# Attention rows in class order: queries, keys, values, bias rows and finished rows, the last pair's sums turned by products, weight splits in halves

## The chip, the cores and the metric

The kernel runs on one core of a Trainium2 chip. The metric is the device time of one execution in microseconds (us); the kernel before takes 1211.53 us, the median of three runs.

## What is computed

One decoder layer on 1024 rows of 1024 numbers: a projection feeds a dilated attention of eight heads and a gated recurrence (HGRN2) of four heads; their outputs are joined, projected, added to x, and a two-layer network with a squared ReLU follows. The part around the change is the attention:

```python
DILATED_PATTERNS = ((128, 1), (512, 4), (2048, 16))
...
def dilated_mixture_attention(q, k, v, slopes):
    outs, lses = [], []
    for window, dilation in DILATED_PATTERNS:
        o, lse = dilated_branch(q, k, v, slopes, window, dilation)
        outs.append(o)
        lses.append(lse)
    w = jax.nn.softmax(jnp.stack(lses, axis=0), axis=0)
    return jnp.sum(w[..., None] * jnp.stack(outs, axis=0), axis=0)
```

A query sees near keys one by one, and farther keys only in steps of 4. A row's *class* is its number modulo 4 (`DIL`): far keys of a query are those of its class.

## The kernel before

Products of fp32 numbers are made of three passes (`three_pass`, L89): each operand is split into a high part, copied by ACT, and the rest, subtracted on DVE (`split_into`, L85). Weights stream through two raw buffers: `w_split` (L110) takes the next tile, ACT writes its high part, DVE its low part, and SP then issues the load of the next but one. `w_get(i, ahead)` (L132) splits up to tile i + ahead. For the output weights the gain is folded in (L124, L125).

The program is recorded in order, each engine runs its own instructions in that order, and waits are made from the data and from the buffers. It has three stages: the four recurrence heads (to about 300 us), the attention (to about 520 us), and the output projection with the two-layer network. All of PE's long work lies in one queue of generators; `fill` (L179) takes pieces from it between the pieces of attention, so that PE has projections to run while other engines work.

The attention of eight heads is a loop of 64 steps (L1275), eight per head: `ITEMS` (L1269) are four diagonal blocks D0 to D3 of the first 512 queries, two far steps F0, F1 and two near steps N0, N1 of the last 512. A step raises the next item's scores to exponentials (`raise_`, ACT), looks at later scores (`look`: products on PE into tile ps, bias and minimum on DVE, a D3 look being 512 columns wide), turns its own block by PE (`turn`: tile pt, then high part pth on ACT and rest ptl on DVE), weighs values with what the step before turned (`weigh`: tile pov), and finishes what was weighed before (`finish`: o on DVE). `fill` runs in the middle and at the end; `hooks` (L1243) adds work of certain steps: splits of output weights, and `row_turn`, which turns finished rows of the recurrence (tile pmt, split into emt).

Two heads share one projection, a *pair*. `attn_proj` (L738) makes queries, values and keys of a pair in two halves of 512 rows: rows are scaled by rrow (the row's norm), written to a half buffer (qf, vf, kf; two such buffers, `half`, L60), split by ACT and POOL (q and ql, kh and kl), and parts are copied across by DMA. Keys and values are put in class order when they are scaled; queries and rrow stand in row order. So far queries are gathered with a step of four (`far_queries`, L860), the near scores' turned tile pt_N is read with a step of four (L929), and the far output is added to row order (L987, L1002). Far denominators reach row order through DRAM (`send`, `receive`), the minimum over both kinds by a small product (`swap_low`, tile px) with picking tiles pick4 and pick32.

When a pair is done, `pair_turn` (tile pot, two halves) and `pair_rows` (anat) bring it back to rows and store it (L1035). This happens in the first three steps of the next pair (L1294, L1327 to L1331). The last pair (`LASTP`) is turned and scaled inside `finish` (L1011 to L1017). PSUM tiles take turns in pairs of banks by tag; pot, pt and pmt share the two of tag t.

## Time and profile before

| | us |
|---|---|
| median of 3 runs (1211.53 to 1212.24) | 1211.53 |
| the profiled execution | 1211.33 |
| its span | 1209.5 |
| PE busy in the span | 1196.5 |
| DVE busy | 861.4 |
| ACT busy | 548.8 |
| POOL busy | 307.4 |

The granted clock of TensorE is full in the whole span. PE's matmuls are pipelined and their ends are modelled, so a busy PE is read with care: a 512-column matmul is shown with 0.39 us, but in an unbroken row the next begins about 0.23 us after it. The idle time of another engine costs nothing as long as PE has work.

### The profile page before, as it was taken

The page shows a single profiled execution, that of the slowest core. Times are in us where ns is not written, and L with a number is a line of the kernel's source. Part 1 is how long each engine was busy: PE and PEld are TensorE (multiplying, and loading weights), DVE is VectorE, ACT ScalarE, POOL GpSimd, SP SyncE. Part 2 cuts the span into 40 slices and gives each one's busy share as a digit, 9 for nine tenths or more (in the row PEclk, how much of TensorE's full clock was granted, in tenths as well). Part 3 has the DMA queues.
Part 4 walks back from the last instruction along what each step waited for, and adds up shares of the span by engine and source line. Part 5 has one row for each costly group of instructions (what it writes and reads, how often), then busy time and mean ns, then how long its engine had stood idle before and what let it go on. Part 6 is the DMA issues. An engine that isn't in the chain of part 4 may idle for free.

```text
span 1209.5 us, 17110 instructions
## 1 busy us (share of the span) xinstructions
PE 1196.5 (99%) x6326; PEld 1023.9 (85%) x6326; DVE 861.4 (71%) x1436; ACT 548.8 (45%) x1067; POOL 307.4 (25%) x287
## 2 busy tenths in 40 slices
PE   9999999999999998999999999999999999999998
PEld 8898989888888887888888888888888888888886
DVE  5697878777667767676689566766678554478796
ACT  7633333322665667765664222222234543534562
POOL 0120212022221110144330786575631000000022
PEclk9999999999999999999999999999999999999999
DMA  5231323123544446173514555553587534433337
GB/s 219 70 93 58 97 83 97 48 82 87 139 99 118 126 124 163 42 243 116 192 61 157 183 194 192 202 182 143 203 320 261 207 100 143 161 100 104 105 105 278
DMA packets 86467, 172.38 MB, mean 143 GB/s; under 512 B 13424, under 2 KB 39024, under 8 KB 86384
## 3 DMA queue, kind: packets, MB, share of 16 engines
q1 hardware_dynamic: 86384, 171.29, 43.5%
q8 instruction: 50, 0.82, 0.3%
q14 instruction: 33, 0.27, 0.1%
HBM read 116.98 MB, written 47.99 MB: 136 GB/s over the span
## 4 chain that ended last, share of the span: by engine, by line
PE 95%; ACT 2%; DVE 1%; issue 1%; DMA 0%; SPq 0%; POOL 0%; DVEq 0%; POOLq 0%; ACTq 0%
PE f L1976 18%; PE f2s L1976 7%; PE pig L92 2%; PE pig L90 2%; PE pig L91 2%; PE pl L488 2%; PE pwo L91 2%; PE pwo L92 2%; PE pwo L90 2%; PE pm_f L90 1%; PE pm_ak L90 1%; PE pm_f L92 1%; PE pm_aq L90 1%; PE pm_f L91 1%; PE pm_aq L92 1%; PE pm_ak L92 1%
## 5 line engine op out<-in xcount | busy, mean ns | idle before, releaser
L87 DVE TENSOR_TENSOR al<-ar,ah 128x1024 fp32r<-128x1024 f32 x56 | 70.6, 1261 | 80.0 <-ACT ah L86 77.6
L1976 PE MATMUL f<-bh,ah 128*128 128x512 f32 x320 | 124.5, 389 | 0.0
L1976 PE MATMUL f<-bl,ah 128*128 128x512 f32 x320 | 124.5, 389 | 0.0
L1976 PE MATMUL f<-bh,al 128*128 128x512 f32 x320 | 124.5, 389 | 0.0
L86 ACT ACTIVATE ah<-ar 128x1024 fp32r<-128x1024 f32 x56 | 59.2, 1057 | 86.9 <-DMA ar<-actd 86.0
L1976 PEld LDWEIGHTS f<-bh,al 128*128 128x128 f32 x320 | 60.1, 188 | 12.6
L1976 PEld LDWEIGHTS f<-bh,ah 128*128 128x128 f32 x320 | 60.1, 188 | 12.5
L1976 PEld LDWEIGHTS f<-bl,ah 128*128 128x128 f32 x320 | 60.1, 188 | 12.3
L2050 POOL TENSOR_SCALAR lbl<-ssq 128x1 f32<-128x1 f32 x4 | 3.3, 821 | 244.9 <-ACT fd L2046 244.8
L1599 POOL TENSOR_TENSOR e<-x,e 128x512 f32<-128x512 f32 x14 | 21.6, 1540 | 131.8 <-DVE x L1550 131.8
L1976 PE MATMUL f2s<-bh,al 128*128 128x512 f32 (+1 forms) x128 | 48.9, 382 | 0.0
L1976 PE MATMUL f2s<-bl,ah 128*128 128x512 f32 (+1 forms) x128 | 48.9, 382 | 0.0
L1976 PE MATMUL f2s<-bh,ah 128*128 128x512 f32 (+1 forms) x128 | 48.9, 382 | 0.0
L717 POOL TENSOR_TENSOR kl<-kf,kh 64x512 fp32r<-64x512 f32 x16 | 22.2, 1391 | 97.0 <-ACT kh L716 82.1
L681 POOL TENSOR_SCALAR tout<-traw 128x256 f32<-128x256 f32 x16 | 19.1, 1196 | 103.1 <-DMA traw<-in_bias_tab_dram 72.1
L87 DVE TENSOR_TENSOR bl<-br,bh 128x1024 fp32r<-128x1024 f32 x32 | 40.1, 1253 | 1.6 <-ACT bh L86 1.5
L1993 ACT ACTIVATE acc<-f 128x512 f32<-128x512 f32 x28 | 16.7, 598 | 48.7 <-PE f L1976 48.7
L761 POOL TENSOR_TENSOR ql<-qf,q 64x512 fp32r<-64x512 f32 x16 | 21.4, 1337 | 62.8 <-ACT q L760 62.2
L86 ACT ACTIVATE bh<-br 128x1024 fp32r<-128x1024 f32 x32 | 33.6, 1050 | 4.8 <-PE f L1976 4.2
L87 DVE TENSOR_TENSOR wl<-raw,wh 128x1024 fp32r<-128x1024 f32 x21 | 25.9, 1233 | 9.1 <-ACT wh L86 9.1
L90 PE MATMUL pwo<-woh,mt 128*128 128x512 f32 x80 | 32.2, 402 | 0.0
L91 PE MATMUL pwo<-wol,mt 128*128 128x512 f32 x80 | 31.3, 391 | 0.0
(1706 smaller groups left out, 3966.5 us busy)
## 6 DMA issues: line engine op xcount, KB each, us to landing
ar<-actd SPq DMA_DIRECT2D x56, 512.0 KB, 3.6
br<-in_w_ff_dram SPq DMA_DIRECT2D x16, 1024.0 KB, 6.0
w1r<-in_w_ff_dram SPq DMA_DIRECT2D x14, 1024.0 KB, 6.5
raw<-in_w_in_dram SPq DMA_DIRECT2D x26, 512.0 KB, 3.7
actd<-e SPq DMA_DIRECT2D x17, 768.0 KB, 4.2
actd<-e SPq DMA_DIRECT2D x11, 1024.0 KB, 4.1
raw<-in_w_out_dram SPq DMA_DIRECT2D x8, 512.0 KB, 4.0
xres<-in_x_dram SPq DMA_DIRECT2D x8, 512.0 KB, 4.5
```

Source lines behind the costliest of these rows:

```text
L86: S.activation(hi, src, AF.Copy)
L87: eng.tensor_tensor(out=lo, in0=src, in1=f32(hi), op=ALU.subtract)
L90: TE.matmul(dst, lhs[0], rhs[0], start=start, stop=False)
L91: TE.matmul(dst, lhs[0], rhs[1], start=False, stop=False)
L92: TE.matmul(dst, lhs[1], rhs[0], start=False, stop=stop)
L488: TE.matmul(pl[:, n % 2, :192], kt[:, n * P:(n + 1) * P], sets[u // 2][:, n % 4], start=True, stop=True)
L681: G.tensor_scalar(by_class(dst[:, part_ * w:(part_ + 1) * w]), in_blocks(raw[:, FAR * DIL:]), -1.0, None, op0=ALU.mult)
L717: G.tensor_tensor(out=kl[a:b], in0=src, in1=f32(kh[a:b]), op=ALU.subtract)
L761: G.tensor_tensor(out=lo[a:b], in0=full[a:b], in1=f32(stacks[i]["q"][a:b, sl]), op=ALU.subtract)
L1599: eng[0].tensor_tensor(out=e1[:, 3], in0=a21, in1=e1[:, 2], op=ALU.add)
L1976: TE.matmul(pm, a[:, j, c], b[:, j, d], start=start and j == 0 and q == 0, stop=stop and j == 1 and q == 2, skip_group_check=True)
L1993: S.activation(acc_at(p, i), pm, AF.Copy)
```

## The change

Queries of a block of 128 rows now stand in class order, like the keys and values. The row scale rrow is put in class order once, in place, by ACT, while pair 0's queries are projected (a copy to a half buffer, a copy back, for each half). Bias rows are loaded in class order by four DMAs for one, the far denominators are received by four, and a finished pair's rows are stored in row order by four. `far_queries` and the near tiles then read runs of 32. The last pair returns to row order inside `weigh`, and its sums by a product with a permuting tile (`in_order`), whose tile POOL makes from the identity.

The order of the steps changes too: at the pair ends `turn` comes before the second `pair_turn`, and the second `pair_rows` directly after `finish`; `far_queries` comes after `finish`; at step 42 the weight split comes before the key copy; two weight splits (steps 48 and 55) are made in halves in two steps (`wo_half`).

```diff
+    def wo_half(k, c):
+        i = WO0 + k
+        sl = slice(c * 512, c * 512 + 512)
...
+        gain = gcols[:, k:k + 1]
+        S.activation(parts[i][0][:, sl], raws[i][:, sl], AF.Copy, scale=gain)
+        V.scalar_tensor_tensor(parts[i][1][:, sl], raws[i][:, sl], gain, f32(parts[i][0][:, sl]),
+                               op0=ALU.mult, op1=ALU.subtract)
+        if c == 1:
+            raws.pop(i)
+            done[1] += 1
+            w_load()
...
+        near_cols = bias_tab[hd][:, T - NEAR + part_ * w:T - NEAR + (part_ + 1) * w].rearrange("(i r) c -> r i c", r=DIL)
+        for r in range(DIL):
+            nc.sync.dma_start(out=raw[32 * r:32 * r + 32, FAR * DIL:], in_=near_cols[r])
...
-        V.tensor_tensor(out=full.rearrange("p (r m) -> p m r", r=DIL), in0=pm.rearrange("p (m r) -> p m r", r=DIL),
-                        in1=rrow[:, sl].rearrange("p (m r) -> p m r", r=DIL), op=ALU.mult)
+        V.tensor_tensor(out=full.rearrange("p (r m) -> p r m", r=DIL), in0=classes(pm),
+                        in1=rrow[:, sl].rearrange("p (r m) -> p r m", r=DIL), op=ALU.mult)
...
+                if pr == 0 and n == 2:
+                    moved = half(f"rc{hf}")
+                    S.activation(moved.rearrange("p (r m) -> p r m", r=DIL), classes(rrow[:, sl]), AF.Copy)
+                    S.activation(rrow[:, sl], moved, AF.Copy)
...
-            V.scalar_tensor_tensor(full, box[0], -0.125, rrow[:, sl], op0=ALU.mult, op1=ALU.mult)
+            V.scalar_tensor_tensor(full.rearrange("p (r m) -> p r m", r=DIL), classes(box[0]), -0.125,
+                                   rrow[:, sl].rearrange("p (r m) -> p r m", r=DIL), op0=ALU.mult, op1=ALU.mult)
...
-                S.activation(stacks[i]["q"][a:b, sl], full[a:b], AF.Copy)
-                G.tensor_tensor(out=lo[a:b], in0=full[a:b], in1=f32(stacks[i]["q"][a:b, sl]), op=ALU.subtract)
+                src = full[a:b].rearrange("p (r j i) -> p j r i", r=DIL, i=32)
+                S.activation(by_class(stacks[i]["q"][a:b, sl]), src, AF.Copy)
+                G.tensor_tensor(out=by_class(lo[a:b]), in0=src, in1=by_class(f32(stacks[i]["q"][a:b, sl])), op=ALU.subtract)
...
-        S.activation(st["q"], q[:, 512:].rearrange("p (m r) -> p r m", r=DIL), AF.Copy)
+        S.activation(st["q"].rearrange("p r (j i) -> p r j i", i=32),
+                     q[:, 512:].rearrange("p (j r i) -> p r j i", r=DIL, i=32), AF.Copy)
...
-        if kind == "D" and g % 2:
+        if kind == "D" and g % 2 and hd // 2 < LASTP:
             V.reciprocal(st["rd"][:, g - 1:g + 1], st["dn"][:, g - 1:g + 1])
...
+    def in_order(hd, a, b, pS):
+        TE.matmul(pS[:, :b - a], early["order"], stats[hd]["dn"][:, a:b],
+                  start=True, stop=True)
+        return pS[:, :b - a]
...
+        if kind == "D":
+            sums = in_order(hd, b0, b0 + 2, po)
...
+        G.tensor_copy(early["order"].rearrange("p (i r) -> p i r", r=DIL), ident.rearrange("p (r i) -> p i r", r=DIL))
...
-        42: lambda: w_get(WO0, 0),
...
-        48: lambda: [values_turn("t"), w_split()],
-        49: lambda: load_bias(AH - 1),
+        48: lambda: [values_turn("t"), wo_half(3, 0)],
+        49: lambda: [wo_half(3, 1), load_bias(AH - 1)],
...
-        55: lambda: [w_get(WO0 + 4, 0), row_load(0)],
+        55: lambda: [wo_half(4, 0), row_load(0)],
+        56: lambda: wo_half(4, 1),
...
+        turn(hd, kind, g)
+        raise_(*coming, which=(1,))
         if s % 16 == 2 and s > 16:
             pair_turn(s // 16 - 1, 1)
-        turn(hd, kind, g)
-        raise_(*coming, which=(1,))
-        if i == 0:
-            far_queries(hd)
...
+        if s % 16 == 2 and s > 16:
+            pair_rows(s // 16 - 1, 1)
         if i == 0:
+            far_queries(hd)
             spread_low(hd, 0)
...
+        if s == 42:
+            w_get(WO0, 0)
         if i in (1, 2, 3, 6, 7):
             key_job()
```

How the change moves instructions, at three places. ACT, where pair 0's queries begin (wh is a weight tile's high part, q the queries' high parts); before:

```order
L1238 ACTIVATE texp<-nhalf 128x1
L86 ACTIVATE wh_2694<-raw_2454 128x1024
L760 ACTIVATE q_0_2709<-qf_2711 64x512
L760 ACTIVATE q_1_2710<-qf_2711 64x512
L760 ACTIVATE q_0_2709<-qf_2770 64x512
```

and now:

```order
L1289 ACTIVATE texp<-nhalf 128x1
L774 ACTIVATE rc_2732<-rrow 128x512
L775 ACTIVATE rrow<-rc_2732 128x512
L86 ACTIVATE wh_2741<-raw_2498 128x1024
L786 ACTIVATE q_0_2756<-qf_2758 64x512
L786 ACTIVATE q_1_2757<-qf_2758 64x512
L774 ACTIVATE rc_2788<-rrow 128x512
L775 ACTIVATE rrow<-rc_2788 128x512
L786 ACTIVATE q_0_2756<-qf_2820 64x512
```

Two copies of rrow stand ahead of the weight split, two more between the two halves of the queries.

ACT at step 42, where the first output weight is split (kh are keys' high parts, pf exponentials); before:

```order
L716 ACTIVATE kh_1_4636<-kf_4738 64x4x128
L124 ACTIVATE woh_4837<-raw_4361,gcols 128x1024
L905 ACTIVATE pf_4650,stat_4648<-pf_4650,stat_4648 128x192
L944 ACTIVATE pth_2_4817<-pt_D_4854 128x4x128
L905 ACTIVATE pf_4650,stat_4648<-pf_4650,stat_4648 128x192
L716 ACTIVATE kh_0_4634<-kf_4849 64x4x128
```

and now:

```order
L124 ACTIVATE woh_4905<-raw_4426,gcols 128x1024
L736 ACTIVATE kh_1_4704<-kf_4807 64x4x128
L936 ACTIVATE pf_4718,stat_4716<-pf_4718,stat_4716 128x192
L975 ACTIVATE pth_2_4889<-pt_D_4926 128x4x128
L936 ACTIVATE pf_4718,stat_4716<-pf_4718,stat_4716 128x192
L736 ACTIVATE kh_0_4702<-kf_4921 64x4x128
```

The split moved ahead of one key copy.

DVE from step 49 to 51 (wl is the fourth output weight's low part, o the last fold of pair 2, anat its rows, ps_F the far looks' scores); before:

```order
L1002 TENSOR_TENSOR o_4563<-pov_far,pn_4714 64x512
L1031 TENSOR_TENSOR anat_5111<-pot_5112,rd_4316 128x512
L857 ISA pf_4946,stat_4943<-ps_F_5119,bt_4646 128x192
L857 ISA stat_4943 128x1
L857 ISA pf_4946,stat_4943<-ps_F_5119,bt_4646 128x192
L857 ISA stat_4943 128x1
L891 TENSOR_TENSOR stat_4943<-px_0_5109,stat_4943 128x4
L878 TENSOR_TENSOR swap_1_5127<-stat_4943,pick_135 128x4x32
L945 TENSOR_TENSOR ptl_2_5136<-pt_D_5134,pth_2_5135 128x3x128
L87 TENSOR_TENSOR emt_4742<-pmt_0_5151,emt_4742 128x512
L1031 TENSOR_TENSOR anat_5111<-pot_5129,rd_4316 128x512
```

and now:

```order
L1046 TENSOR_TENSOR o_4631<-pov_far,pn_4785 64x512
L141 SCALAR_TENSOR_TENSOR wl_5140<-raw_4976,gcols,wh_5139 128x512
L1079 TENSOR_TENSOR anat_5187<-pot_5188,rd_4378 128x512
L883 ISA pf_5018,stat_5015<-ps_F_5195,bt_4714 128x192
L883 ISA stat_5015 128x1
L883 ISA pf_5018,stat_5015<-ps_F_5195,bt_4714 128x192
L883 ISA stat_5015 128x1
L922 TENSOR_TENSOR stat_5015<-px_0_5185,stat_5015 128x4
L910 TENSOR_TENSOR swap_1_5203<-stat_5015,pick_133 128x128
L976 TENSOR_TENSOR ptl_2_5207<-pt_D_5205,pth_2_5206 128x3x128
L1079 TENSOR_TENSOR anat_5187<-pot_5213,rd_4378 128x512
L87 TENSOR_TENSOR emt_4812<-pmt_0_5232,emt_4812 128x512
```

Half a weight split came in between o and the first anat (the other half stands where the whole one stood, ahead of the D3 look of step 48), and the second anat moved ahead of emt. On PE the three turns of pt_D stand ahead of the second pot now, behind it before.

## Rows read from the trace of the kernel before

**Rows 1.** The page, part 1: busy time and share of the span.

```profile
PE 1196.5 (99%) x6326; PEld 1023.9 (85%) x6326; DVE 861.4 (71%) x1436; ACT 548.8 (45%) x1067; POOL 307.4 (25%) x287
```

**Rows 2.** Windows: stretch, length, busy us of each engine, clock, DMA.

```profile
440.00:460.00 20.00, 18.46 (x112) 15.43 (x110) 14.38 (x44) 14.07 (x36) 3.85 (x3) 1.00 0.51 135
460.00:480.00 20.00, 18.35 (x118) 15.41 (x116) 16.00 (x47) 13.48 (x31) 1.29 (x1) 1.00 0.67 176
480.00:500.00 20.00, 19.58 (x130) 17.29 (x129) 13.83 (x47) 15.25 (x44) 1.41 (x3) 1.00 0.27 73
```

**Rows 3.** The chain of waits, 440 to 480: start us, length us, what.

```profile
449.81 0.64 ACT kh L716
450.46 1.16 ACT woh L124
451.64 1.28 DVE wol L125
452.93 0.97 DVE kf L697
...
470.18 1.29 DVE wl L125
```

**Rows 4.** PE's timeline: start us, busy us, operation, count [idle before <-releaser].

```profile
454.46 0.38 PE L963 MATMUL pov<-ptl,v 128*128 128x256 f32 x1 [0.88 <-DVE ptl L945]
...
474.88 0.52 PE L915 MATMUL pt_D<-ident,pd 128*128 128x128 f32 x3
475.15 0.48 PE L90 MATMUL pwe<-wh,emt 128*128 128x512 f32 x1
...
478.64 0.66 PE L915 MATMUL pt_D<-ident,pd 128*128 128x128 f32 x4 [0.60 <-DVE emt L87]
479.05 0.47 PE L90 MATMUL pwe<-wh,emt 128*128 128x512 f32 x1
```

**Rows 5.** The same view of DVE and of ACT, around step 50.

```profile
474.05 0.69 DVE L1031 TENSOR_TENSOR anat<-pot,rd 128x512 f32<-128x512 f32 x1
...
477.26 0.60 ACT L86 ACTIVATE emt<-pmt 128x512 fp32r<-128x512 f32 x1 [0.28 <-PE pmt L1108]
```

**Rows 6.** The same view of PE, step 55.

```profile
494.37 0.39 PE L852 MATMUL ps_N<-kh,q 128*128 128x256 f32 x1 [0.34 <-DVE stat L857]
```

**Rows 7.** The same view of PE: the small product px and what follows it.

```profile
498.58 0.28 PE L886 MATMUL px<-pick,swap 128*128 128x4 f32 x2
498.72 0.34 PE L852 MATMUL ps_F<-kh,qc 128*128 128x192 f32 x1
```

**Rows 8.** The same view of ACT, DVE, POOL and PE around 255.

```profile
251.64 1.04 ACT L86 ACTIVATE wh<-raw 128x1024 fp32r<-128x1024 f32 x1
...
252.72 1.22 DVE L87 TENSOR_TENSOR wl<-raw,wh 128x1024 fp32r<-128x1024 f32 x1 [1.77 <-ACT wh L86]
...
257.12 1.78 DVE L558 TENSOR_TENSOR qt<-qt,tot 128x512 f32<-128x512 f32 x1
...
255.35 3.00 POOL L761 TENSOR_TENSOR ql<-qf,q 64x512 fp32r<-64x512 f32 x2 [11.02 <-ACT q L760]
...
259.25 1.89 PE L552 MATMUL pl<-qt,kt 128*128 128x64 f32 x16
```

**Rows 9.** Groups by line and shape: count | busy us, mean ns | idle.

```profile
L945 DVE TENSOR_TENSOR ptNl<-pt_N,ptNh 128x512 fp32r<-128x512 f32 x16 | 11.0, 690 | 5.0 <-ACT ptNh L944 4.8
...
L697 DVE TENSOR_TENSOR kf<-pm_ak,rrow 128x512 f32<-128x512 f32 x6 | 6.4, 1072 | 0.0
...
L945 DVE TENSOR_TENSOR ptl<-pt_D,pth 128x512 fp32r<-128x512 f32 x8 | 5.5, 689 | 11.7 <-ACT pth L944 11.7
...
L864 ACT ACTIVATE qc<-q 128x512 fp32r<-128x512 f32 x8 | 9.0, 1129 | 0.0
...
L717 POOL TENSOR_TENSOR kl<-kf,kh 64x512 fp32r<-64x512 f32 x16 | 22.2, 1391 | 97.0 <-ACT kh L716 82.1 <-PE ps_N L853 14.7
L681 POOL TENSOR_SCALAR tout<-traw 128x256 f32<-128x256 f32 x16 | 19.1, 1196 | 103.1 <-DMA traw<-in_bias_tab_dram 72.1 <-issue 31.0
```

More of the change, by code (lines that the diff above doesn't have):

```diff
@@ L130, in w_split @@
             w_load()
+    def wo_half(k, c):
+        i = WO0 + k
+        sl = slice(c * 512, c * 512 + 512)
+        if c == 0:
+            hl = stream[i][1]
+            parts[i] = hl() if hl else (wp.tile([P, T], F32R, tag="wh", name=f"wh{i}", bufs=2),
+                                        wp.tile([P, T], F32R, tag="wl", name=f"wl{i}", bufs=2))
+        gain = gcols[:, k:k + 1]
[6 more added lines that the diff above has]
+            w_load()
     def w_get(i, ahead=1):
@@ L240, in hymba_layer @@
     nc.sync.dma_start(out=mraw, in_=level_masks)
-    pick4 = [cp.tile([P, DIL], F32, name=f"pick4{i}") for i in range(2)]
-    pick32 = [cp.tile([P, 32], F32, name=f"pick32{i}") for i in range(2)]
+    pick4 = cp.tile([P, DIL], F32, name="pick4")
+    pick32 = cp.tile([P, 32], F32, name="pick32")
     mix_dram = dp.tile([T, D], F32, name="mixd")
@@ L869, in receive @@
     def receive(hd):
+        if hd // 2 < LASTP:
+            for r in range(DIL):
+                nc.sync.dma_start(out=stats[hd]["xd"][32 * r:32 * r + 32],
+                                  in_=swap_dram[hd].rearrange("(j i) r -> r i j", i=32)[r])
+            return
         nc.sync.dma_start(out=stats[hd]["xd"],
@@ L877, in spread_low @@
         src = stats[hd]["least"][:, 8:12] if far else stats[hd]["least"][:, 4:8]
-        V.tensor_tensor(out=z if not far else z.rearrange("p r i -> p (r i)").rearrange("p (i r) -> p r i", r=DIL),
-                        in0=src.unsqueeze(2).to_broadcast([P, DIL, 32]),
-                        in1=pick32[far].unsqueeze(1).to_broadcast([P, DIL, 32]), op=ALU.mult)
+        V.tensor_tensor(out=z, in0=src.unsqueeze(2).to_broadcast([P, DIL, 32]),
+                        in1=pick32.unsqueeze(1).to_broadcast([P, DIL, 32]), op=ALU.mult)
         swapped[hd, far] = z
@@ L885, in swap_low @@
         pS = swapped[hd, far] = bank("s", f"px{hd}_{far}")
-        TE.matmul(pS[:, :DIL], z, pick4[far], start=True, stop=True)
+        TE.matmul(pS[:, :DIL], z, pick4, start=True, stop=True)
     def joint(hd, far):
@@ L965, in weigh @@
             ot = stats[hd]["D"][1] if g == 0 else stats[hd]["D"][3][:, :256]
-            S.activation(ot[mine], po[other, :256], AF.Copy)
+            if hd // 2 == LASTP:
+                S.activation(ot.rearrange("p (b i r) -> p b i r", b=2, r=DIL),
+                             po[:, :256].rearrange("p (b r i) -> p b i r", b=2, r=DIL), AF.Copy)
+            else:
+                S.activation(ot[mine], po[other, :256], AF.Copy)
             return po, ot
@@ L992, in finish @@
         if kind == "N":
-            V.tensor_tensor(out=st["xd"], in0=st["dn"][:, 4:8], in1=st["xd"], op=ALU.add)
+            sums = st["dn"][:, 4:8] if pr < LASTP else in_order(hd, 4, 8, bank("s", f"pd{hd}"))
+            V.tensor_tensor(out=st["xd"], in0=sums, in1=st["xd"], op=ALU.add)
             V.reciprocal(st["rd"][:, 4:], st["xd"])
@@ L1016, in finish @@
         V.tensor_reduce(dst, pair.rearrange("p u a d -> p u d a"), axis=AX.X, op=ALU.add)
+        if kind == "D":
+            V.reciprocal(st["rd"][:, b], sums)
         G.tensor_tensor(out=dst, in0=dst, in1=st["rd"][:, b].unsqueeze(2).to_broadcast([P, n, 64]), op=ALU.mult)
@@ L1034, in pair_rows @@
         if hf == 1:
-            nc.sync.dma_start(out=mix_dram[:, AW + pr * P:AW + (pr + 1) * P].rearrange("(n p) d -> p n d", p=P),
-                              in_=anats[pr].rearrange("p n i d -> p n (i d)"))
+            to = mix_dram[:, AW + pr * P:AW + (pr + 1) * P].rearrange("(n i r) d -> r i n d", r=DIL, i=32)
+            for r in range(DIL):
+                nc.sync.dma_start(out=to[r], in_=anats[pr][32 * r:32 * r + 32].rearrange("p n i d -> p n (i d)"))
     rows, xress, mts, pmo, gains, scales = {}, {}, {}, {}, {}, {}
@@ L1053, in early_rows @@
         early["table"] = wide.tile([P, 2, T], F32, tag="A", name="etable")
+        early["order"] = early["table"][:, 1, :P]
+        G.tensor_copy(early["order"].rearrange("p (i r) -> p i r", r=DIL), ident.rearrange("p (r i) -> p i r", r=DIL))
         early["mt"] = [wide.tile([P, 2, 2, 4, P], F32R, tag="A", name=f"emt{q}") for q in range(NE // 2)]
```

35 lines of the change are left out of this document (18 added, 17 removed).

## The prediction

> **What bounds the kernel now.** I read the page first: PE is busy for 1196.5 of 1209.5 us [rows 1], so the other engines matter only where PE waits for them. Next the busy time by windows, to find those places. PE stands idle for 1.54 us between 440 and 460, 1.65 us between 460 and 480 and 0.42 us between 480 and 500 [rows 2]: 3.6 us in the last third of attention, and almost nothing after it. That is the kernel's last pair of heads, where splits of the output weights stand among the splits and folds of attention. Any saving on DVE, ACT, POOL or SP outside such a place is worth nothing by itself; any PE work or any new PE wait counts in full. The chain of waits [rows 3] says what PE waits for there: an ACT copy, an ACT split, the DVE split that needs it, then a key product. PE's own timeline [rows 4] gives the size of the single waits in brackets.
>
> The profiled execution took 1211.33 us, 0.2 us under the median of the three runs (1211.53), with 1209.5 of it in the span. The sum below is made against 1211.33, and what lies outside the span is left as it is. 0.2% of it, about what a measurement can tell from no change, is 2.4 us.
>
> **The change, part by part.** Clock times are those of the kernel before; each term assumes the earlier ones only shift the clock.
>
> (a) *The row scale put in class order: +1.4 us.* Each half of rrow is copied to class order and back by two ACT instructions. On ACT the first two now stand directly ahead of the split of a weight tile at 251.64. The first copy reads SBUF with a step of four elements; the nearest row is the far-query copy, 128x512 with that step, 1.13 us [rows 9]. The copy back runs straight; by the 512-column kh copy it takes 0.64 us [rows 3]. The second needs the first, so the weight split starts about 1.7 us late. DVE had waited 1.77 us for that split, and everything behind it on DVE moves with it: wl at 252.72, and at the end of an unbroken row of instructions qt, which ends at 257.12 + 1.78 = 258.90 [rows 8]. PE reads qt at 259.25 [rows 8]. With 258.90 + 1.7 = 260.6 it waits 1.35 us, and PE has nothing else in its queue. Bounds: 0, if the step costs ACT nothing and DVE catches up; 1.9, if PE's slack of 0.35 us is no slack at all. I take 1.4. The second pair of copies waits for POOL's products on the half buffer, but DVE asks for its result only later; 0.
>
> (b) *Step 42, weight split ahead of the key copy: -0.9 us.* The ACT copy kh (449.81, 0.64 us) stood ahead of woh (450.46); wol (451.64) and kf (452.93) follow on DVE [rows 3], ptl behind kf, and PE waits 0.88 us for ptl until 454.46 [rows 4]. Without kh in front all of it comes 0.64 us earlier, and kf, which now reads rrow straight and writes straight, falls from 1.07 us to the 0.69 us of a straight product [rows 9]: 0.64 + 0.38 = 1.02, of which the wait holds 0.88. Bounds: 0, if ACT merely moves its queue (kh then stands ahead of the exponentials), and -1.0. I take -0.9. The ACT work behind it moves by about as much, so the lead should last.
>
> (c) *Steps 48 to 51: -1.0 us.* The split of the fourth weight tile is one DVE instruction of 1.29 us at 470.18 [rows 3], ahead of the D3 look and of all that leads to anat at 474.05 [rows 5]. Now half of it stands there, about 0.65 us; it starts some 0.3 us earlier because ACT too does only half first. So the look and what follows come 0.9 us earlier. The other half then stands between o and anat and takes 0.6 back: anat ends about 0.35 us earlier, near 474.4. PE's pt_D now goes ahead of pot and needs no wait; pot takes the bank that anat frees, at 474.4, and four turns last 0.41 us (478.64 to 479.05), so the next projection starts near 474.8 instead of 475.15 [rows 4]: -0.35. From there to 478.64 PE had 2.9 us of its own and then waited 0.60 us for emt [rows 4]. The next pt_D now waits for the second anat, which has moved ahead of emt on DVE, so the 0.60 goes: 474.8 + 2.9 = 477.7, 0.95 us early. ACT, almost without a gap from its emt at 477.26 on [rows 5], starts that queue earlier by as much. Bounds: +0.1, if anat ends where it did, and pot's turns now follow it instead of pt_D's three; -2.0, near the 1.65 us of idle time between 460 and 480 [rows 2] and what hides in modelled ends. I take -1.0.
>
> (d) *Steps 55 and 56, the same halves: -0.3 us.* PE waits 0.34 us for looks that stand behind a whole split of a weight tile on DVE [rows 6]. With half of it in front, some 0.65 us less, that wait goes; the other half then stands before the D3 look and delays it a little. Bounds: 0, if what goes in front comes back behind, and -0.5, with the start-up around the wait.
>
> (e) *Six products that put sums in order: +0.8 us.* Each head of the last pair gets three, an fp32 product with 2 or 4 columns. The nearest row is px, 4 columns, two PE instructions: 498.58 to 498.72, 0.14 us until the next start [rows 7]. 6 x 0.14 = 0.84. Bounds: 0, if they fall into waits; 1.3, if the matmul behind each loses 0.07 as well.
>
> (f) *pot behind pt_D at the two earlier pair ends: +0.1 us.* There pt_D no longer waits for anat and pot does, with four turns for three. Bounds 0 and 0.5.
>
> (g) *At nothing:* the straight products for keys and values and the copy of the far queries free DVE and ACT, off PE's path. The extra DMAs (bias rows, denominators, finished rows, each four for one) cost SP some 0.4 us a piece; the loads that they delay are issued microseconds ahead. If that cover went, a weight tile would come up to 1.2 us late, once a head. POOL's copy that makes the order tile is done before the key products that queue behind it. The reciprocal behind the sums delays only POOL.
>
> Sum: 1.4 - 0.9 - 1.0 - 0.3 + 0.8 + 0.1 = 0.1, so 1211.4.
>
> *A rule weighed.* qf, kf and vf now read PSUM with a step of four elements. The turned near tile was read so before, and its product takes 690 ns against 689 ns of the straight one [rows 9]: the step costs DVE nothing. The Trainium skill (SBUF - State Buffer, "Door 1: The DMA port swizzle") says that PSUM has 8-byte lines and that non-contiguous patterns there slow matmuls significantly, and gives SBUF 16-byte lines. On PSUM read by DVE the trace does not bear it out; it is the last rival.
>
> **The rivals.**
> - *Faster: the waits go nearly all.* Class order shortens what DVE and ACT do all through this stretch, and the 3.6 us of idle time [rows 2] vanish, with the six products inside what is left of them; (a) costs 1.0 because the step costs ACT less. -3.6 + 1.0 = -2.6: 1208.7. For it: every wait there has an edit of its own. Against it: DVE and ACT are busy for 14 to 16 of 20 us there [rows 2], and a lead on PE soon meets one of them. 13%.
> - *Slower: POOL holds DVE at 255.* kt and qt take far longer than the 0.69 us of such products while POOL computes ql (qt 1.78 us [rows 8]). POOL now reads qf in 16 runs instead of one. POOL's product with a step of four takes 1196 ns for 256 columns, kl in runs of 128 takes 1391 ns for 512 [rows 9]: 1.7 times as long per column. If the short runs cost that and more, so that the two products take 6 us instead of 3.00 [rows 8], qt ends up to 3 us later still and PE waits for it: 1214.4. It decides from about 1.2 us more per product. Against it: a run of 32 is far from a step of four, and kl already works in runs. 12%.
> - *The lead is lost again.* ACT and DVE need their time in these steps whatever the order; (b), (c) and (d) give nothing, and 1.4 + 0.8 + 0.1 stay: 1213.6. 16%.
> - *The step in PSUM costs DVE* what it costs kf in SBUF, 0.38 us: (a) grows by that, (b) loses as much: 1212.2. The Trainium skill's rule on lines would make it so. The rows above speak against it. 4%.
>
> **How the numbers follow.** Forecast 55%, 1211.4, with its own bounds 1209.5 to 1213. The range gives up half of the fast and most of the slow rival: 1208.9 to 1213.7. Faster by over 0.2%: the first rival and a tail of the forecast, 0.15. Slower: POOL's hold and some of the lost lead, 0.15. Within: 0.70.
>
> **What would show it.** Right: (a) two ACT copies of 1.1 and 0.6 us at 251.6 and a PE wait above 1 us near 259 before the second pl; (b) no PE wait for ptl near 454; (c) pot waiting for anat, pt_D of step 51 at least 0.8 us earlier against the clock of (b); (e) six pairs of short PE instructions. PE's idle time between 440 and 500 should fall from 3.6 to about 1.5 us. Wrong, if PE shows no wait near 259, if the idle time between 440 and 500 is as large as before or nearly gone, or if ql takes over 2 us.

## The result and the profile after

The changed kernel takes 1213.62 us, the median of 22 executions, against 1211.70 for the kernel before, also of 22: a ratio of 1.0015, with a 95% interval of 1.0009 to 1.0022. That is 1.9 us slower (1.1 to 2.7), 0.16%. It lies just inside the range given (1208.9 to 1213.7), but above the forecast's own bounds (1209.5 to 1213): the forecast of 1211.4 was practically no change, 0.1 us above the profiled execution of before. The profiled execution of the changed kernel took 1212.77 us, with 1211.0 in the span: 1.5 us more than the span before. So two things are to be explained: 1.5 us between the two traces where the sum had 0.1, and a median that stands 0.85 above its own profiled execution where that of before (1211.70 and 1211.33) stands 0.37 above.

The page's first part answers to [rows 1], the windows to the three of [rows 2]:

```profile
PE 1197.1 (99%) x6338; PEld 1025.0 (85%) x6338; DVE 854.5 (71%) x1436; ACT 548.9 (45%) x1073; POOL 306.9 (25%) x288
```

```profile
440.00:460.00 20.00, 19.69 (x120) 16.86 (x119) 13.76 (x45) 13.15 (x36) 4.24 (x3) 1.00 0.55 142
460.00:480.00 20.00, 18.02 (x120) 15.63 (x119) 17.05 (x49) 13.63 (x35) 1.29 (x1) 1.00 0.56 142
480.00:500.00 20.00, 19.67 (x131) 17.23 (x130) 13.25 (x45) 15.70 (x48) 0.80 (x2) 1.00 0.31 89
```

PE's idle time between 440 and 460 fell from 1.54 to 0.31 us, between 460 and 480 it rose from 1.65 to 1.98, between 480 and 500 it fell from 0.42 to 0.33. In sum 2.62 instead of 3.6 us: less than before, more than the 1.5 forecast.

To see where the time went I read **the lag**: the start of a PE instruction in the trace of the changed kernel, less the start of the same instruction before. PE's timeline of the changed kernel at the steps (start, busy time, line, operation, tiles, count, and in brackets the idle time ahead):

```profile
260.66 2.00 PE L576 MATMUL pl<-qt,kt 128*128 128x64 f32 x16 [1.18 <-DVE qt L582]
...
281.50 1.97 PE L576 MATMUL pl<-qt,kt 128*128 128x64 f32 x16 [0.62 <-DVE tot L586]
...
424.12 0.48 PE L90 MATMUL pm_aq<-hTh,wh 128*128 128x512 f32 x1
...
456.15 0.36 PE L994 MATMUL pov<-ptl,v 128*128 128x256 f32 x1
...
474.50 0.49 PE L946 MATMUL pt_D<-ident,pd 128*128 128x128 f32 x3
476.47 0.66 PE L1075 MATMUL pot<-ident,o 128*128 128x128 f32 x4 [1.48 <-DVE anat L1079]
476.88 0.47 PE L90 MATMUL pwe<-wh,emt 128*128 128x512 f32 x1
479.36 0.63 PE L946 MATMUL pt_D<-ident,pd 128*128 128x128 f32 x4
...
495.00 0.33 PE L878 MATMUL ps_N<-kh,q 128*128 128x256 f32 x1
498.43 0.38 PE L1029 MATMUL pd<-stat,etable 128*128 128x4 f32 x2 [0.24 <-DVE stat L883]
...
518.41 0.63 PE L1058 MATMUL pov_far<-ident,pn 128*128 128x128 f32 x4
```

The same instructions before began at 259.25, 454.46, 475.15, 478.64 and 494.37 [rows 4, 6, 8], and at 279.19, 421.59 and 516.86. The differences, from one to the next:

| stretch (clock of before) | lag from, to | it adds | forecast |
|---|---|---|---|
| up to the second pl, 259 (a) | 0.02, 1.41 | +1.39 | +1.4 |
| to the pl at 279 (g, held at nothing) | 1.53, 2.31 | +0.78 | 0 |
| to 422, with two pair ends (f) | 2.31, 2.54 | +0.23 | +0.1 |
| to ptl at 454 (b) | 2.54, 1.69 | -0.85 | -0.9 |
| to pt_D at 479 (c) | 1.69, 0.72 | -0.97 | -1.0 |
| to ps_N at 494 without the products (d) | 1.08, 0.63 | -0.45 | -0.3 |
| the products, 479 to 517 (e) | 0.72, 1.08 and 0.63, 1.55 | +1.28 | +0.8 |

Between 259 and 279 the lag drifts from 1.41 to 1.53, behind 517 it settles at 1.3, and the span ends 1.5 later. (a), (b), (c) and (d) came within 0.15 us of what was forecast, each where it was forecast. Two lines did not: the 0.78 at 279, and the products. Run 10 below shows that (d) and the products belong together.

ACT, DVE and their order near 255 show (a) as the prediction had it, copies of 1.09 and 0.63 us ahead of the weight split, which starts 1.74 us later than the 251.64 of [rows 8]; PE waits 1.18 us for qt:

```profile
251.71 1.09 ACT L774 ACTIVATE rc<-rrow 128x512 f32<-128x512 f32 x1
252.84 0.63 ACT L775 ACTIVATE rrow<-rc 128x512 f32<-128x512 f32 x1
253.38 1.04 ACT L86 ACTIVATE wh<-raw 128x1024 fp32r<-128x1024 f32 x1
254.45 1.23 DVE L87 TENSOR_TENSOR wl<-raw,wh 128x1024 fp32r<-128x1024 f32 x1 [3.44 <-ACT wh L86]
...
258.84 1.76 DVE L582 TENSOR_TENSOR qt<-qt,tot 128x512 f32<-128x512 f32 x1
```

The 0.78 us at 279 is the lesson of this case. First the trace of before there, DVE, POOL and PE (kf is pair 0's first key product, kl what POOL makes of it, kt and qt are products of the recurrence that PE's pl needs):

```profile
274.87 1.06 DVE L697 TENSOR_TENSOR kf<-pm_ak,rrow 128x512 f32<-128x512 f32 x1 [0.76 <-PE pm_ak L92]
276.60 0.69 DVE L556 TENSOR_TENSOR kt<-kt,tot 128x512 f32<-128x512 f32 x1 [0.67 <-PE pl L552]
276.67 3.46 POOL L717 TENSOR_TENSOR kl<-kf,kh 64x512 fp32r<-64x512 f32 x2 [11.61 <-ACT kh L716]
277.21 1.78 DVE L558 TENSOR_TENSOR qt<-qt,tot 128x512 f32<-128x512 f32 x1
278.91 1.26 DVE L562 TENSOR_TENSOR tot<-tot 128x32 f32<-128x32 f32 x1
279.19 1.91 PE L552 MATMUL pl<-qt,kt 128*128 128x64 f32 x16
```

and the changed kernel's:

```profile
276.39 0.69 DVE L717 TENSOR_TENSOR kf<-pm_ak,rrow 128x512 f32<-128x512 f32 x1 [0.78 <-PE pm_ak L92]
277.82 2.98 POOL L737 TENSOR_TENSOR kl<-kf,kh 64x512 fp32r<-64x512 f32 x2 [11.11 <-ACT kh L736]
278.12 1.52 DVE L580 TENSOR_TENSOR kt<-kt,tot 128x512 f32<-128x512 f32 x1 [1.04 <-PE pl L576]
279.57 1.78 DVE L582 TENSOR_TENSOR qt<-qt,tot 128x512 f32<-128x512 f32 x1
281.27 0.18 DVE L586 TENSOR_TENSOR tot<-tot 128x32 f32<-128x32 f32 x1
```

kf fell from 1.06 to 0.69 us, as was meant. So ACT copies kh 0.37 us sooner, and POOL starts kl sooner. Before, DVE's kt started 0.07 us ahead of kl and took 0.69 us. Now kl starts 0.30 us ahead of kt, and kt takes 1.52 us. qt took 1.78 us behind it either way, so against PE's clock it ends 0.8 us later, at 281.35, and PE starts pl at 281.50 after a wait of 0.62 us. The row of PE names tot as what it waited for, but pl reads qt and kt alone, and in the trace of before it began at 279.19 while tot still ran (278.91 to 280.17): what it waits for is qt. A DVE instruction became 0.37 us faster, and the next one lost twice as much.

The Trainium skill (SBUF — State Buffer, "Who interferes with whom") says that DVE with two inputs in SBUF and GpSimd, when it reads SBUF, use one port in turn, and that issue order decides which of them waits. The trace agrees as far as the order goes: 0.69 us for kt when it is first, 1.52 when it is second.

The last part is the clock. Here are the windows and PE's timeline of an execution of another kernel that has the same wait at 259 us (the one with whole splits, below), in the columns of the fences above; in the windows the granted clock stands behind the busy times:

```profile
255.00:260.00 5.00, 4.33 (x20) 3.23 (x19) 5.00 (x6) 1.30 (x3) 2.90 (x2) 1.00 0.44 129
260.00:265.00 5.00, 4.47 (x22) 3.99 (x23) 5.00 (x7) 3.84 (x5) 1.45 (x1) 0.73 0.36 100
265.00:270.00 5.00, 5.00 (x30) 4.33 (x29) 3.32 (x5) 0.21 (x1) 1.50 (x2) 0.93 0.46 106
```

```profile
260.53 2.10 PE L576 MATMUL pl<-qt,kt 128*128 128x64 f32 x16 [1.20 <-DVE qt L582]
262.96 0.63 PE L91 MATMUL pm_av<-hTl,wh 128*128 128x512 f32 x1
263.39 0.63 PE L92 MATMUL pm_av<-hTh,wl 128*128 128x512 f32 x1
263.81 0.63 PE L90 MATMUL pm_av<-hTh,wh 128*128 128x512 f32 x1
...
265.84 0.39 PE L92 MATMUL pm_av<-hTh,wl 128*128 128x512 f32 x1
266.07 0.39 PE L90 MATMUL pm_av<-hTh,wh 128*128 128x512 f32 x1
```

The granted clock is 1.00, then 0.73 and 0.93, then 1.00 again. PE waits 1.20 us for qt; behind that its 512-column matmuls begin 0.42 to 0.43 us apart, where they are 0.23 apart at full clock. That is the lower of the two levels, 1.2 GHz for 2.4, and it goes on to 265.5. The lag rises there by another 1.6 us. In the profiled execution of the changed kernel the clock stayed full. Of its 22 executions ten have a mean clock of at most 0.998 over the span and a median of 1214.7 us; the other twelve have a median of 1213.0, 1.3 above before, close to the 1.4 of the table. So the wait has a second price, which one profile shows or doesn't show.

### The profile page after: what moved, and what is told of

It is laid out like the page before. It is cut to its first block, busy times and chain, and to the rows that moved or that the text cites. A ratio compares the mean times of both kernels' runs of the same rounds, so it can differ in the third digit from the quotient of the medians.

```text
span 1211.0 us, 17270 instructions
## 1 busy us (share of the span) xinstructions
PE 1197.1 (99%) x6338; PEld 1025.0 (85%) x6338; DVE 854.5 (71%) x1436; ACT 548.9 (45%) x1073; POOL 306.9 (25%) x288
## 4 chain that ended last, share of the span: by engine, by line
PE 75%; ACT 1%; DVE 1%; issue 1%; POOL 0%; DVEq 0%; POOLq 0%; ACTq 0%
PE f L2028 18%; PE f2s L2028 7%; PE pwo L90 2%; PE pwo L92 2%; PE pwo L91 2%; PE pm_ak L90 1%; PE pm_av L90 1%; PE pm_ak L92 1%; PE pm_ak L91 1%; PE pm_av L92 1%; PE pm_av L91 1%; PE pm_aq L90 1%; PE pl L576 1%; PE pm_aq L92 1%; PE pm_aq L91 1%; PE pov L994 1%
## 5 line engine op out<-in xcount | busy, mean ns | idle before, releaser
L90 PE MATMUL pwo<-woh,mt 128*128 128x512 f32 x80 | 32.2, 402 | 0.0
L92 PE MATMUL pwo<-woh,mt 128*128 128x512 f32 x80 | 31.2, 390 | 0.0
```

The source lines that it names most:

```text
L90: TE.matmul(dst, lhs[0], rhs[0], start=start, stop=False)
L92: TE.matmul(dst, lhs[1], rhs[0], start=False, stop=stop)
```

## The experiments

Each kernel was run 11 times beside the kernel before (15 to 33 executions, 1211.62 to 1211.87 us); lags are read at the same instructions as above. "At most 0.998" counts executions with such a mean clock over the whole span. It tells executions with a fall from others only roughly, since the end of a span has a lower clock too (0.62 from 1205 us on in the trace of before, where PE is idle): of the executions of the kernel before in these series, 11 of 108 have such a clock.

**1. The changed kernel again.** No edit.

> The changed kernel once more, beside the others. Against before the profile of the first run counted +1.4 at 259 us, +0.85 at 280, +0.2 at the two earlier pair ends, -0.9 at step 42, -1.0 at steps 48 to 51, -0.45 at step 55 and some +1.2 for the six products: +1.3. If these sizes are the kernel's own and not that run's, each comes back within 0.15 us, and the time is 1.5 to 2 us above before.

Measured: 1214.20 us, ratio 1.0019 (1.0010 to 1.0028). Each stretch came back as in the table, within 0.03 us, up to the wait for anat: +1.36 at 259, +0.78 at 279, +0.23 at the pair ends, -0.85 at step 42. At 475 this profile shows a fall of the clock behind the wait of pot:

```profile
470.00:475.00 5.00, 5.00 (x34) 4.21 (x32) 4.26 (x17) 4.57 (x10) 0.00 (x0) 1.00 0.48 100
475.00:480.00 5.00, 3.52 (x18) 2.99 (x16) 4.04 (x11) 0.49 (x1) 0.00 (x0) 0.72 0.69 198
480.00:485.00 5.00, 5.00 (x36) 4.56 (x35) 1.85 (x5) 4.27 (x13) 0.40 (x1) 0.94 0.91 262
```

0.72 and 0.94 of full clock; the lag at pt_D near 479 is 3.02, not 1.4 as it would be with the -0.97 of the table. So one fall costs 1.6 us. Eight of the 11 executions have a mean clock of at most 0.998. The sizes are the kernel's own. The start of the span shifts the lag by up to 0.75 us from one execution to another (0.02 at 10 us in the first profile, 0.75 in this one), which is why I subtract lags.

**2. The key product of pair 0 made slow again.** Only the order in which its elements are walked differs, in scale and result.

```diff
-        V.tensor_tensor(out=full.rearrange("p (r m) -> p r m", r=DIL), in0=classes(pm),
-                        in1=rrow[:, sl].rearrange("p (r m) -> p r m", r=DIL), op=ALU.mult)
+        form = "p (r m) -> p m r" if pr == 0 else "p (r m) -> p r m"
+        V.tensor_tensor(out=full.rearrange(form, r=DIL),
+                        in0=pm.rearrange("p (m r) -> p m r", r=DIL) if pr == 0 else classes(pm),
+                        in1=rrow[:, sl].rearrange(form, r=DIL), op=ALU.mult)
```

> Pair 0's key product is made in row order again: the same numbers, but its scale and its result have a step of four in SBUF, so it should take 1.07 us as before and not 0.69. Theory (POOL overtakes): the shorter product let POOL's kl start before DVE's kt near 278, and kt then took 1.52 us instead of 0.69; with the slower product kt goes first, the 0.8 us wait of PE for pl near 281 is gone, and the kernel gets about 0.85 us faster than the changed one, although one of its instructions is slower. Rival (the second copy of the row scale, or the shift of 1.4 us, made that wait): the wait stays, and the time is the changed kernel's, or 0.4 us more.

Measured: 1212.23 us, ratio 1.0005 (0.9996 to 1.0014), 2.0 us under the changed kernel beside it.

```profile
277.00 1.05 DVE L718 TENSOR_TENSOR kf<-pm_ak,rrow 128x512 f32<-128x512 f32 x1 [0.78 <-PE pm_ak L92]
278.73 0.69 DVE L580 TENSOR_TENSOR kt<-kt,tot 128x512 f32<-128x512 f32 x1 [0.68 <-PE pl L576]
278.80 3.46 POOL L739 TENSOR_TENSOR kl<-kf,kh 64x512 fp32r<-64x512 f32 x2 [11.47 <-ACT kh L738]
...
281.32 1.91 PE L576 MATMUL pl<-qt,kt 128*128 128x64 f32 x16
```

kt is 0.07 us ahead of kl again, takes 0.69 us, and pl at 281.32 has no wait ahead; the lag passes 279 without a step (2.13 ahead of it and behind it). This settles the 0.78: POOL's lead, not the second pair of copies, made that wait. The rest of the 2.0 us goes with the clock: two of 11 executions at most 0.998 here, eight of 11 in run 1. Why the wait at 259, which is still there, was followed by a fall less often in this run, the run does not tell.

**3. The first copies of the row scale on DVE.**

```diff
+                    if hf == 0:
+                        V.tensor_copy(moved.rearrange("p (r m) -> p r m", r=DIL), classes(rrow[:, sl]))
+                        V.tensor_copy(rrow[:, sl], moved)
```

> The first pair of copies of the row scale is made by DVE, which stood idle for 1.8 us there in the kernel before, instead of ACT; the second pair stays on ACT. Theory (the copies on ACT delay the weight split): the split goes at 251.7 again, PE's wait of 1.2 us near 259 goes down to at most 0.3, the kernel gets 1.1 to 1.4 us faster than the changed one. Rival (DVE is the one that binds there): DVE's copies push wl and qt as far as ACT's did, and the wait stays above 1 us.

Measured: 1211.71 us, ratio 0.9999 (0.9990 to 1.0008), 2.5 us under the changed kernel.

```profile
251.03 0.61 DVE L775 COPY rc<-rrow 128x512 f32<-128x512 f32 x1
251.67 0.43 DVE L776 COPY rrow<-rc 128x512 f32<-128x512 f32 x1
251.81 1.04 ACT L86 ACTIVATE wh<-raw 128x1024 fp32r<-128x1024 f32 x1
252.88 1.23 DVE L87 TENSOR_TENSOR wl<-raw,wh 128x1024 fp32r<-128x1024 f32 x1 [0.78 <-ACT wh L86]
...
259.39 1.89 PE L576 MATMUL pl<-qt,kt 128*128 128x64 f32 x16
```

DVE makes both copies in 1.04 us, in time in which it waited before [rows 8]. pl has no wait at 259 (lag 0.14 there, 0.16 at 10 us); the 0.79 at 279 and all else stay. One of 11 executions has a clock of at most 0.998. The wait is worth 1.39 us by the lag, and the median moved by more: the falls went with it.

**4. Both edits.**

> Both edits. If the two costs are separate, the sum of both gains, about 2.1 us: the kernel stands some 0.5 us below before or equal to it (1211.2 to 1211.9 where before has 1211.7). If both were one wait seen twice, or if the next late step takes the lead back before 440 us, the gain is that of the larger edit alone, 1.2 to 1.4.

Measured: 1210.54 us, ratio 0.9991 (0.9983 to 1.0000). The lag is 0.12 at 259 and 0.13 on both sides of 279: neither step is left. The two costs are separate and add up: near 597 the lag is -0.94, in the changed kernel's first profile, which has no fall, 1.32; that is 2.3 us for the 1.39 + 0.78 of the two steps. The median fell by more than that, 3.66 us beside run 1, and is 0.7 under the lower end of what I had expected: two of 11 executions are at most 0.998, in run 1 eight.

**5. The second half of the fourth weight's split behind anat.**

```diff
-        49: lambda: [wo_half(3, 1), load_bias(AH - 1)],
+        49: lambda: load_bias(AH - 1),
...
             pair_rows(s // 16 - 1, 0)
+            if s == 49:
+                wo_half(3, 1)
```

> In the changed kernel, the second half of the fourth output weight's split (DVE 0.75 us) stands behind the first anat, not ahead of it. In the changed kernel PE waits 1.48 us for that anat, with pot, near 475 us. Theory: the wait falls to about 0.75, the lag to before falls by 0.7 to 0.75 from there on; and since in one of two profiles of the changed kernel the granted clock fell right behind that wait (0.72 from 475 to 480) and cost 1.6 us more, runs with a clock of 0.998 and a span above 1212 become rare, so that the median falls by more than 0.75, to between 1212.0 and 1212.9. Rival for the clock: it falls because of something else, and half of the runs stay 1.5 us above the fastest ones. Rival for the wait: PE then waits for the weight's second half instead, and nothing is gained.

Measured: 1213.13 us, ratio 1.0012 (1.0003 to 1.0021): missed. pot's wait fell from 1.48 to 0.70 us, but a new one of 0.32 came behind it:

```profile
477.85 0.66 PE L1075 MATMUL pot<-ident,o 128*128 128x128 f32 x4 [0.70 <-DVE anat L1079]
479.92 0.66 PE L1159 MATMUL pmt<-ident,erows 128*128 128x128 f32 x4 [0.32 <-DVE ptl L976]
```

The stretch to pt_D gave -1.23 for -0.97, so 0.26 us were gained and not 0.75: DVE owed the same work a little later. And the clock still fell in some executions (six of 11 at most 0.998); the profiled one shows it at 261 to 267 us, behind the wait at 259, with 1.6 us. I had looked for the falls at the wrong wait.

**6. Without the six products.**

```diff
-        TE.matmul(pS[:, :b - a], early["order"], stats[hd]["dn"][:, a:b],
-                  start=True, stop=True)
-        return pS[:, :b - a]
+        return stats[hd]["dn"][:, a:b]
```

> The changed kernel without its six products that put the last pair's sums in order: the sums are taken in class order as they are, so the last pair's rows are scaled by the sums of other rows. The prediction had 0.14 us a product, 0.84 together. By the first profile of the changed kernel they cost 1.1 to 1.3 from 479 to 517 us, one of them (the first with four columns, near 498) with a wait of 0.24 for a bank. Theory: PE pays the products in full, 1.0 to 1.3 us back. Rival: they fall into waits for DVE that come back when they go, 0.5 or less.

Measured: 1212.53 us, ratio 1.0007 (0.9999 to 1.0016). From 479 to 517 the lag goes from 0.77 to 0.33 here, from 0.72 to 1.55 in the changed kernel: the products cost 1.27 us, and no wait comes back in their place. In the lag the first one with four columns adds 0.64 alone (0.58 to 1.22), with a wait of 0.24 us for DVE to leave its bank (the row at 498.43 above) and a slow start behind it. (1.27 - 0.64) / 5 = 0.13 is left for each of the other five. Why DVE is late there, run 10 shows.

**7. The old order at the pair ends.**

```diff
+        if s % 16 == 2 and s > 16:
+            pair_turn(s // 16 - 1, 1)
         turn(hd, kind, g)
         raise_(*coming, which=(1,))
-        if s % 16 == 2 and s > 16:
-            pair_turn(s // 16 - 1, 1)
...
-        if s % 16 == 2 and s > 16:
-            pair_rows(s // 16 - 1, 1)
...
+        elif s % 16 == 2 and s > 16:
+            pair_rows(s // 16 - 1, 1)
```

> The changed kernel with the old order at the pair ends: the second pot ahead of the turns of pt_D, the second anat at the end of the step, so behind emt; the halves of the splits stay. Theory: the order made the gain near 479 us: pt_D waits for emt again there, the lag rises by some 0.75, pot waits as long as before for the first anat, and the two earlier pair ends give back 0.2; so 0.4 to 0.7 us slower than the changed kernel. Rival: the halves made the gain, and the order costs or gives nothing: within 0.2 of it.

Measured: 1214.57 us, ratio 1.0023 (1.0014 to 1.0031). The stretch from 454 to 479 adds 0.02 where the changed kernel has -0.97; the earlier pair ends add 0.13 for 0.23. So the order is worth 0.99 us at the last pair and costs 0.1 at the others: term (c) is the order's, with anat ahead of emt, and the wait of pt_D for emt is back at 0.60 us, the number of [rows 4]. In sum that is 0.9 us by the lag, more than the 0.4 to 0.7 expected.

**8. Both edits, and the second pot behind a piece of a projection.**

```diff
-        if s % 16 == 2 and s > 16:
-            pair_turn(s // 16 - 1, 1)
...
         for _ in range(units // 2):
             fill(0.0, True)
+        if s % 16 == 2 and s > 16:
+            pair_turn(s // 16 - 1, 1)
```

> Copies of the row scale on DVE, the slow key product of pair 0, and the second pot behind the next piece of a projection instead of ahead of it, at all three pair ends. That piece lasts 0.7 us on PE, so pot should wait no more at 367 and 421 us (0.85 and 0.56 before) and 0.7 less near 475; the pieces of the projection do not wait for pot. Expected: 2.0 us less than with the two edits alone, about 1208.5, 0.25% below before. Rival: what pot releases (anat, and the bank of the next turn) is then late and PE waits behind it: 0 to 1 us less.

Measured: 1209.70 us, ratio 0.9983 (0.9974 to 0.9992). The two earlier pair ends give -0.99 where they cost 0.23, but 0.44 of that is lost again, as the stretch to 454 gives only -0.41 for -0.85; at 475 pot still waits 0.78 us for anat (1.49 in run 4) and pmt 0.35 for ptl, so that the stretch to pt_D gives -1.11 for the -0.96 of run 4. 0.84 us gained of the 2.0 expected, no execution at most 0.998, and all 11 within 1.0 us.

**9. In addition the second half of that split behind the second anat, in step 50.**

```diff
-        49: lambda: [wo_half(3, 1), load_bias(AH - 1)],
+        49: lambda: load_bias(AH - 1),
...
         if s % 16 == 2 and s > 16:
             pair_rows(s // 16 - 1, 1)
+        if s == 50:
+            wo_half(3, 1)
```

> The last best kernel (copies on DVE, slow key product, second pot behind a piece of the projection) with the second half of the fourth output weight's split, on ACT and DVE, in step 50 behind the second anat. PE first reads that half 1.3 us after the first one, in the next block of columns. Theory: the first anat then follows o directly, so pot's wait of 0.78 us and the 0.35 for pmt behind it go, 1.0 us less than the last best one: about 1208.7. Rival, as where the half was only moved behind the first anat (0.28 us gained of 0.75): DVE owes the same work, and PE waits for the half itself or for emt: within 0.3 of it.

Measured: 1208.87 us, ratio 0.9978 (0.9969 to 0.9987): 2.9 us faster than before, faster than both kernels. From 454 to 597 us the lag falls by 1.26, in run 8 by 0.54: 0.7 us gained of the 1.0 expected. PE has no wait ahead of pot any more; 0.34 us are left for pmt, behind ptl. That half could wait until here because the first block of columns doesn't read it: its DVE part runs from 474.75 to 475.50, and PE's next block of columns begins at 475.69.

**10. The weight splits whole again.**

```diff
-        48: lambda: [values_turn("t"), wo_half(3, 0)],
-        49: lambda: [wo_half(3, 1), load_bias(AH - 1)],
+        48: lambda: [values_turn("t"), w_split()],
+        49: lambda: load_bias(AH - 1),
...
-        55: lambda: [wo_half(4, 0), row_load(0)],
-        56: lambda: wo_half(4, 1),
+        55: lambda: [w_get(WO0 + 4, 0), row_load(0)],
```

> The changed kernel with both weight splits whole again, at steps 48 and 55; the order at the pair ends stays new. Theory: the first half of step 48 brings the looks earlier but the second half takes it back before anat, so that the lag to before is up by 0.6 to 0.8 near 473 us and back near 475; the half of step 55 gives 0.45. So 0.4 to 0.6 us slower than the changed kernel. Rival, the forecast's view that half of the split behind o leaves anat 0.35 earlier: 0.8 to 1.0 slower. Second rival: 0.

Measured: 1214.43 us, ratio 1.0020 (1.0011 to 1.0029). The stretch to 479 gives -0.78 for -0.97, that to 494 nothing for -0.45: up to 494 the halves are worth 0.2 at step 48 and 0.45 at step 55, 0.64 together. The forecast had put 0.35 of (c) on half a split less ahead of anat; it is 0.2.

But most of the 0.45 does not last. Here the first product with four columns has no wait, and the next PE instruction starts 0.16 us behind it:

```profile
500.24 0.30 PE L1029 MATMUL pd<-stat,etable 128*128 128x4 f32 x2
500.40 0.63 PE L1058 MATMUL pov_far<-ident,pn 128*128 128x128 f32 x4
```

In the changed kernel the other half of the split (step 56) stands on DVE ahead of the D3 look, whose bank that product takes:

```profile
497.02 0.75 DVE L141 SCALAR_TENSOR_TENSOR wol<-raw,gcols,woh 128x512 fp32r<-128x512 f32 x1 [0.19 <-ACT woh L140]
497.69 0.68 DVE L883 CUSTOM_DVE_ANT_0 pd<-ps_D,etable 128x512 f32<-128x512 f32 x1
```

The look ends at 498.30 there, so PE's product at 498.43 has to wait, and it costs 0.64 us in the lag. From 479 to 517, with all six products, the lag rises by 0.90 in this run and by 0.83 in the changed kernel: the half at step 55 is worth 0.07 us in the end, both halves 0.26 from 454 to 517, less than the 0.4 to 0.6 expected.

**11. Step 42's split behind the key copy again.**

```diff
-        if s == 42:
-            w_get(WO0, 0)
...
+        42: lambda: w_get(WO0, 0),
```

> The changed kernel with step 42's weight split behind the key copy again. Theory: the order made the gain of 0.85 us near 455 us, as the copy of 0.63 us stood ahead of the split on ACT and PE waited for what comes behind it; the shorter key product (0.69 for 1.07) gives only the rest: 0.5 to 0.65 us slower than the changed kernel, with PE's wait for ptl back at 0.5 to 0.65. Rival: the shorter key product alone made it: within 0.2.

Measured: 1213.93 us, ratio 1.0022 (1.0014 to 1.0031). The stretch to 454 gives -0.20 for -0.85: the order is worth 0.65 us, nearly the 0.64 of the copy that stood ahead, and the shorter key product the rest. PE's wait for ptl is back at 0.62 us.

**12. The kernel before with the four copies alone.**

```diff
+                if pr == 0 and n == 2:
+                    moved = half(f"rc{hf}")
+                    S.activation(moved.rearrange("p (m r) -> p r m", r=DIL),
+                                 rrow[:, sl].rearrange("p (m r) -> p r m", r=DIL), AF.Copy)
+                    S.activation(rrow[:, sl], moved, AF.Copy)
```

> The kernel before with nothing but the four ACT copies of the row scale at their places (to a half buffer with a step of four, and back; the order stays that of rows, so all else stays too). Theory of the wait: PE waits 1.2 us for qt near 259 and the lag there is 1.35 as in the changed kernel; near 280 no further wait, as the key product is the slow one. Theory of the clock: the wait is enough to let the granted clock fall behind it in some executions; runs at 0.998 or less, 1.5 to 2 us above the others, come in 3 to 7 of 11, and the median stands 1.4 to 2.8 above before. Rival: the clock falls only where the waits of attention follow too, or by chance: all runs within 1.2 us of each other, 1.2 to 1.5 above before.

Measured: 1214.27 us, ratio 1.0022 (1.0013 to 1.0031). The lag is 1.46 from 259 on and 1.59 at 517: nothing is added anywhere else.

```profile
258.80 1.76 DVE L558 TENSOR_TENSOR qt<-qt,tot 128x512 f32<-128x512 f32 x1
260.71 1.97 PE L552 MATMUL pl<-qt,kt 128*128 128x64 f32 x16 [1.28 <-DVE qt L558]
```

Five executions lie between 1212.86 and 1213.69 us with clocks of 0.999 and 1.000, six between 1214.27 and 1215.77, all six at 0.998. So one wait of 1.28 us costs 1.4 us for certain, and in about half of the executions some 2 us more (medians of the two groups: 1213.20 and 1215.22); the median stands 2.65 over before (1211.62). None of the attention's edits is needed for it.

Taken together: the nine series with the wait at 259 us (the first one of the changed kernel, runs 1, 2, 5 to 7 and 10 to 12) have a clock of at most 0.998 in 53 of 110 executions, the four without it (3, 4, 8, 9) in 3 of 44, although two of these four (3 and 4) keep pot's wait of 1.5 us at 475. Within the nine the count goes from two of 11 (run 2) to eight (run 1). In four profiles (runs 5, 7, 10, 11) the clock fell behind the wait at 259, in one (run 1) behind that at 475.

## Why the prediction was wrong

Its main view held: PE bounds the kernel, and only PE's waits and PE's own work count. Point by point:

- **(a)** right in size, place and cause: 1.39 us for 1.4, by the copies of 1.09 and 0.63 us on ACT (runs 3 and 12). That the second pair of copies costs nothing was right too: run 12 shows no further step.
- **(b)** right: -0.85 for -0.9, 0.65 of it by the order (run 11).
- **(c)** right in sum, -0.97 for -1.0, and not quite in its parts: the first anat did not end 0.35 us earlier, and the next projection began no earlier (lag 1.69 at 454, 1.72 at 475). pot's wait was longer than I saw, 1.48 us, because the looks and pt_D ahead of it came early. The order, emt behind anat, gave 0.99 alone (run 7).
- **(d)** right at its place, -0.45 for -0.3, but 0.4 of it comes back 4 us later (run 10). That is its bound 0, "if what goes in front comes back behind".
- **(e)** 1.27 for 0.84 us. Five products cost about the 0.14 us of px; the sixth costs 0.64, because it takes a bank of the looks that DVE still reads, and DVE is late there by the other half of (d)'s split. With whole splits the six cost 0.90 (run 10). I priced the instructions and did not look up which bank each writes.
- **(f)** right: of the 0.23 in its stretch, the order at the pair ends makes 0.1 (run 7).
- **(g), the step that failed**: "the straight products for keys and values [...] free DVE and ACT, off PE's path", at nothing. The first key product of pair 0 stands between two products of the recurrence for which PE waits, and its 0.37 us went to POOL's kl, which then started ahead of DVE's kt: +0.78 us on PE. The prediction had the very mechanism in its second rival, with POOL's ql and DVE at 255, and asked there only whether POOL would take longer. At 276 it was the start that mattered, and with the slow product put back the step is gone (run 2). The two rows that would have told it stood in the trace of before: kt at 276.60, kl at 276.67, 0.07 us apart.
- **The clock** was in no case. The profiled execution of before has no fall, so I priced a wait by its length. Between the two profiled executions the time differs by 1.44 us, between the medians by 1.92. The 0.5 us between the two go with the executions in which the clock fell: the twelve above 0.998 have a median 1.3 over before, and with (a)'s wait as the only change such executions come in six of 11 (run 12). Why the clock falls in some executions and not in others stays open.

The corrected sum is 1.39 + 0.78 + 0.23 - 0.85 - 0.97 - 0.45 + 1.28 = 1.4 us, against 1.5 in the spans. The terms (a) to (d) and (f), each near its place, add up to -0.7 as forecast and to -0.65 as measured; (g) and (e) make the rest. That the time lies inside the range is luck as far as (g) and the clock go, for neither had a place in it.

The rivals: "the waits go nearly all" fell, as 2.62 us of idle time are left. "The lead is lost again" fell for (b) and (c), which gave what they should and kept it, and held for (d) alone; its time of 1213.6 is the one measured, by luck. "The step in PSUM costs DVE" fell: kf, with a step of four in PSUM and none in SBUF, takes 0.69 us. The rule on PSUM's lines that the prediction weighed there (the Trainium skill, SBUF — State Buffer, "Door 1: The DMA port swizzle") speaks of matmuls. For DVE's reads the trace shows no such cost, and on matmuls no run here shows anything. "POOL holds DVE at 255" fell as put: the two ql there take 2.98 us instead of 3.00, so runs of 32 cost POOL nothing. POOL did hold DVE 20 us later, not because it took longer but because it started first.

## What to carry over

When an instruction on one engine gets faster, look at what it releases: if that competes with another engine's next instruction, the two starts decide, and a margin of 0.07 us in the trace is a warning. The wait of 1.2 us at 259 cost PE more than its length, so look at several executions: the time that the clock takes from what follows may be missing from the one that was profiled. Follow a gain to the end of its stretch: the 0.45 us of step 55 were there at 494 and nearly gone at 498. A copy that must be made is best put on an engine that waits there anyway: here DVE, which made in 1.04 us what ACT needed 1.72 for.

## What the runs showed of the hardware

- DVE's two copies of 128x512 fp32 take 0.61 us (reading with a step of four) and 0.43 us (straight), ACT's 1.09 and 0.63. The DVE product with a step of four in its scale and result in SBUF takes 1.05 us; with the step in PSUM alone, 0.69.
- POOL's product in 16 runs of 32 takes as long as in one run: ql 2.98 us for two, 3.00 before.
- The order of two starts 0.07 and 0.30 us apart decided whether a DVE product of 128x512 took 0.69 or 1.52 us (DVE first by 0.07 in the kernel before and run 2, POOL first by 0.30 in the changed kernel); POOL's pair took 3.46 us when DVE was first and 2.98 when POOL was.
- TensorE's granted clock fell to the lower level behind a wait of 1.2 to 1.3 us of an otherwise busy PE (profiles of runs 5, 7, 10 and 11), and a fall took 1.6 us by the lag, about 2 in the medians of run 12. The mean clock over the span was at most 0.998 in 53 of 110 executions with that wait and in 3 of 44 without it.
